# Reading scanned states in place in an S5 layer's output products

## The chip, the cores and the metric

The kernel runs on one core of one Trainium2 chip. The metric is device time in microseconds (us), from the start of the program to its end. A profiled execution also gives a trace with the instructions of each engine: PE (TensorE, with its weight loads as PEld), ACT (ScalarE), DVE (VectorE), POOL (GpSimd) and SP (SyncE, which issues most of the DMAs).

## The reference, cut to what matters

The program is an encoder of two layers on 256 tokens of width 2048, in float32. The first layer is attention; the change doesn't touch it. The second is a bidirectional S5 state-space layer, with a projection, a complex scan in each direction, an output product, a GELU, a gated unit and an output projection:

```
proj = einsum('bsd,de->bse', h, w_in);  u, z = split(proj, 2)
ug = u.reshape(b, s, 128 groups, 16 channels)
y_fwd = s5_direction(ug, ..., False);  y_bwd = s5_direction(ug, ..., True)
y = y_fwd + y_bwd + d_skip * u
g = gelu(y)
y = g * sigmoid(einsum('bse,ef->bsf', g, w_glu) + b_glu) * silu(z)
return einsum('bse,ed->bsd', y, w_out)
# s5_direction, with a state of 64 complex numbers per group:
bu = einsum('sbgc,gpc->sbgp', u, bb);  s[t] = a * s[t-1] + bu[t]
return einsum('gcp,sbgp->sbgc', c_re, s_re) - einsum('gcp,sbgp->sbgc', c_im, s_im)
```

## The kernel before

**Large products.** Each weight matrix is read in chunks of 512 KB. SP issues the load into `raw` (five buffers), ACT casts it into the high part `wh` (L146, three buffers), and POOL or DVE subtracts to get the low part `wl` (L148). PE then multiplies high by high, high by low and low by high: 24 matmuls with 256 columns for a chunk (L209 to L211). The S5 layer begins with 64 such chunks on `h1T`: four per block of 256 outputs, for u in chunks 0 to 31 and for the gate z in chunks 32 to 63. The GLU follows on `gT`, from chunk 64. Its first two blocks are interleaved: chunks 64 to 69 are quarters 0 to 2 of both, and chunk 70 is quarter 3 of the first, which needs the results of pieces 12 to 15. In chunks 1 to 69 it is POOL that makes `wl`. Six chunks of the last product (`w_out_ssm`) are loaded and split ahead of time into `kept`.

**The scan in pieces.** The sequence is cut into 64 slots of four tokens. The 128 groups form 16 pieces of eight. For each block of u, `ut` goes to DRAM (`Ud`, L841 and L842), and comes back as the right operand of `in_products` (L871), where PE makes the contributions of each slot to the states with 64x64 matmuls in four quarters of its array. ACT copies them into `V` (L875). `V` is laid out by slot, part (real or imaginary) and group, with one tile for pieces 0 to 7 and one for 8 to 15. The forward states lie on partitions 0 to 63, the backward states, with the order of the slots reversed, on 64 to 127. `scan_task` runs twice on DVE, once for each tile: per slot one product with the coefficients (L888) and two additions (L889, L890), each slot after the one before it.

**The outputs.** `out_task` makes one piece's outputs after its scan. Two copies (L908 on ACT; L909 on ACT, from piece 8 on DVE) and two memsets on POOL bring the states of the piece into `su`, shifted by a slot and with the backward part turned round. Sixteen matmuls `om` by `su` over 128 rows and eight `tt` by `up2` over 64 rows (L933) sum states and inputs in one bank of PSUM. ACT applies the GELU (L938) and issues the store to `Gd`; `g_task` reads that back as `gp` and splits it into `gT` (L243, L244). `tt` is a rearranged copy (L498) of eight 64 KB loads `tr` for every four pieces.

**What sets the order.** After each chunk a `step` advances the generators of the lanes in, scan, out and g, each by a step or a few. The out lane holds two tasks (`OUT_W`). The scan takes three slots per step. The `out_task`s of eight pieces are queued four steps (`OUT_LAG`) after their scan was written out, and a `g_task` waits in addition until no scan is left. A scheduler then puts each engine's instructions in one fixed order. Where an instruction waits, everything behind it on its engine waits too. `PSB` divides PSUM: three banks for the chunks, three for the pieces.

Of the kernel before, what the change touches and what calls it, by code (L numbers as in the profile page):

```python
# [18 lines left out]
S = 256  # L19
# [5 lines left out]
G = 128  # L25
# [15 lines left out]
class Trunk:  # L41
# [241 lines left out]
    def ssm_tables(self, tp, pp):  # L283
# [98 lines left out]
        self.coef = self.const.tile([128, 2, 2, G], F32, name="coef")  # L382
        nc.gpsimd.tensor_copy(self.coef[:, 0], pw[4][0].unsqueeze(1).to_broadcast([128, 2, G]))
        nc.gpsimd.tensor_copy(self.coef[:, 1, 0], pw[4][1])
        v.tensor_scalar(self.coef[:, 1, 1], pw[4][1], -1.0, None, ALU.mult)
# [101 lines left out]
    def toeplitz(self, b):  # L487

        nc, wk = self.nc, self.wk1
        raw = wk.tile([128, L, 16, C], F32, tag="q4", name="tr", bufs=self.Q4)  # L490
        with self.tc.issue_after(self.paced):
            for h in range(2):
                for tau in range(L):
                    src = self.Kd[b, h, :, 3 - tau:7 - tau].rearrange("c j e -> c (j e)")
                    nc.sync.dma_start(raw[h * 64 + tau:h * 64 + 64:L].rearrange("q j a e -> q (j a e)"), src)
        t = wk.tile([128, 16, C, L], F32, tag="tt", name="tt")
# [347 lines left out]
    def in_task(self, pc):  # L844
# [11 lines left out]
            yield  # L856
        self.small.append(lambda: self.in_products(pc, im, up))

    def in_products(self, pc, im, up):
        if pc == 8:  # L860
            self.V.append(self.s1.tile([128, NCH, 2, 64], F32, tag="s1", name="V"))
        nc, V, g0 = self.nc, self.V[pc // 8], pc % 8 * PG

        pss = [self.bank("vps").rearrange("p (g r s) -> p g r s", g=4, r=2) for _ in range(2)]
        with self.urgent() if self.IN_URG else ExitStack(), ExitStack() as order:
            for pr in range(4):
                for ri in range(2):
                    for hf, d in ((0, 0), (1, 1), (0, 1), (1, 0)):
                        h = slice(hf * 64, hf * 64 + 64)
                        mv = up[h, 1, pr] if d == 0 else up[h, 0, pr, ::-1]  # L870
                        m = nc.tensor.matmul(pss[hf][d * 64:d * 64 + 64, pr, ri], lhsT=im[h, pr, ri, d * 64:d * 64 + 64], rhs=mv, start=True, stop=True)  # L871
                        order.enter_context(self.tc.issue_after(m.ins))
        with self.urgent():
            for hf in range(2):
                nc.scalar.copy(V[:, :, :, g0 + hf:g0 + PG:2].rearrange("p s r g -> p g r s"), pss[hf])  # L875
        self.flags.add(("V", pc))

    def scan_task(self, p0, p1):

        v = self.nc.vector  # L880
        n, g0 = (p1 - p0) * PG, p0 % 8 * PG
        V = self.V[p0 // 8][:, :, :, g0:g0 + n]
        cf = self.coef[:, :, :, p0 * PG:p1 * PG]
        shp = [128, 2, 2, n]
        for c in range(1, NCH - 1):
            P = self.sc.tile([128, 512], F32, tag="scp", name="scp")[:, :4 * n].rearrange("q (e r g) -> q e r g", e=2, r=2)
            with self.urgent():
                v.tensor_tensor(P, cf, V[:, c - 1].unsqueeze(1).to_broadcast(shp), ALU.mult)  # L888
                v.tensor_tensor(V[:, c], V[:, c], P[:, 0], ALU.add)  # L889
                self.swept = v.tensor_tensor(V[:, c], V[:, c], P[:, 1, ::-1], ALU.add).ins  # L890
            yield
        t = self.now + self.OUT_LAG
        while self.now < t:
            yield
        for pc in range(p0, p1):
            self.add("out", self.out_task(pc))

    def out_task(self, pc):

        nc, v, wk = self.nc, self.nc.vector, self.wk1  # L900
        b, q = pc // 4, pc % 4
        V = self.V[pc // 8]
        gs = slice(pc % 8 * PG, pc % 8 * PG + PG)
        su = wk.tile([128, 2, PG, NCH], F32, tag="q4", name="su", bufs=self.Q4)
        f, r = slice(0, 64), slice(64, 128)
        nc.gpsimd.memset(su[f, :, :, 0:1], 0.0)  # L906
        nc.gpsimd.memset(su[r, :, :, NCH - 1:], 0.0)
        nc.scalar.copy(su[f, :, :, 1:], V[f, 0:NCH - 1, :, gs].rearrange("p s r g -> p r g s"))  # L908
        (v.tensor_copy if pc >= 8 else nc.scalar.copy)(su[r, :, :, :NCH - 1], V[r, NCH - 2::-1, :, gs].rearrange("p s r g -> p r g s"))  # L909
        self.flags.add(("su", pc))  # L910
        tag, bufs = ("im", self.NIM) if self.n_in == NPIECE and self.OMT else ("q4", self.Q4)
        om = wk.tile([128, 2, PG, C * L], F32, tag=tag, name="om", bufs=bufs)
        nc.sync.dma_start(om, self.OMd[pc])
        if q == 0:
            self.tt = self.toeplitz(b)
        tt = self.tt
        up = wk.tile([128, 4, NCH], F32, tag="up", name="up2", bufs=3)
        nc.sync.dma_start(up, self.Ud[pc].rearrange("h c t a k -> (h c t) a k"))
        yield
        yield  # L920
        ps = self.pm.tile([128, 512], F32, tag="pm", name="yps", bufs=self.npm)

        h = [slice(g % 2 * 64, g % 2 * 64 + 64) for g in range(PG)]
        o = [ps[h[g], g // 2 * NCH:g // 2 * NCH + NCH] for g in range(PG)]
        even, odd = range(0, PG, 2), range(1, PG, 2)
        jobs = [(g, None) for g in even] + [(g, ri) for ri in range(2) for g in range(PG)] + [(g, None) for g in odd]
        seen = set()
        with ExitStack() as order:
            for n, (g, ri) in enumerate(jobs):
                lhsT = tt[h[g], q * 4 + g // 2].rearrange("q e t -> q (e t)") if ri is None else om[:, ri, g]  # L930
                rhs = up[h[g], g // 2] if ri is None else su[:, ri, g]
                stop = ri is None if g % 2 else ri == 1
                m = nc.tensor.matmul(o[g], lhsT=lhsT, rhs=rhs, start=g % 2 not in seen, stop=stop, skip_group_check=True)  # L933
                seen.add(g % 2)
                order.enter_context(self.tc.issue_after(m.ins))
# [4 lines left out]
        self.add("g", self.g_task(pc), *[("su", p) for p in range(8)])  # L940

    def g_task(self, pc):

        nc, wk = self.nc, self.wk1
        yield

        while not self.idle("scan"):
            yield

        if self.gT is None:  # L950
            self.gT = self.s2.tile([128, 2, KB, S], F32R, tag="s2", name="gT")
        gp = wk.tile([128, S], F32, tag="gp", name="gp", bufs=6)
        nc.sync.dma_start(gp, self.Gd[pc].rearrange("g c t k -> (g c) (t k)"))
        for _ in range(self.GLAG):
            yield
        with self.tc.issue_after(self.mm) if self.GLAG > 2 else ExitStack(), self.tc.issue_after(self.swept):
            self.split(gp, self.gT[:, 0, pc], self.gT[:, 1, pc])
        self.flags.add(("g", pc))

    def glu_task(self, f, src, dst):  # L960
# [4 lines left out]
        gg = wk.tile([128, S], F32, tag="gp", name="gg", bufs=6)  # L965
# [7 lines left out]
    def open(self, ssm):  # L973
# [6 lines left out]
        cf = self.sc.tile([128, 2, 2, G], F32, name="cf")  # L980
        self.nc.scalar.copy(cf, self.coef)
        self.coef = cf
        self.V = [self.s2.tile([128, NCH, 2, 64], F32, tag="s2", name="V")]
        p0 = 0
        for p1 in self.BATCH:
            self.add("scan", self.scan_task(p0, p1), *[("V", p) for p in range(p0, p1)])
            p0 = p1
        self.flags.add("open")

    def layer1(self, out):  # L990
# [5 lines left out]
        self.gT, self.n_in = None, 0  # L996
# [135 lines left out]
    EACH = 2
# [56 lines left out]
```

## Time and profile before

| what | value |
|---|---|
| median of 3 runs | 916.02 us (911.74 to 917.16) |
| the profiled execution's own time | 910.61 us |
| its span | 908.4 us, so 2.2 us lie around it |
| mean granted clock of TensorE | 0.978 of full speed |
| busy share of the span | PE 93%, DVE 72%, ACT 57%, POOL 29% |
| HBM | 214 GB/s over the span |

Busy shares are means over stages of different kinds. The S5 layer's u blocks start a new piece about every four chunks from 440 us on. The last piece's `in_products` end at 560.8 us, and chunk 70 begins at 728.6 us; between these two the scans end and all outputs are made.

### The profile page before, as it was taken

What the parts mean: (1) busy time and instruction counts of PE and PEld (TensorE: products, weight loads), DVE (VectorE), ACT (ScalarE), POOL (GpSimd) and SP (SyncE); (2) the same over time, 40 slices, a digit from 0 to 9 for tenths busy, and PEclk for the clock granted to TensorE, in tenths of its full rate; (3) what the DMA queues carried; (4) which work ended last, traced back from release to release, by engine and by line L of the source; (5) the groups of instructions that cost most, each with busy time, mean ns of one, the idle gap of its engine ahead of it and who ended that gap; (6) DMA issues with size and microseconds to landing.
All of it is one profiled execution on the core that took longest, in us unless ns stands there. A gap on an engine that the chain in (4) does not pass through costs nothing.

```text
span 908.4 us, 18403 instructions
## 1 busy us (share of the span) xinstructions
PE 841.9 (93%) x7244; PEld 759.0 (84%) x7244; DVE 658.4 (72%) x1178; ACT 520.3 (57%) x743; POOL 263.4 (29%) x182
## 2 busy tenths in 40 slices
PE   5999999999999999997999999998898799999993
PEld 4788889989899787786889999987898699988872
DVE  3999899899979979967300798999632388756546
ACT  3554457778667674344566556489869464443321
POOL 0008500000001324433756666733684000000004
PEclk9999999999999999998999999998999989999997
DMA  9765587777767567987799899756886936777723
GB/s 228 239 192 180 142 255 212 246 187 227 187 199 199 181 178 235 240 280 251 234 261 272 256 290 283 198 152 179 241 257 206 314 123 210 231 237 242 236 50 92
DMA packets 217798, 195.82 MB, mean 216 GB/s; under 512 B 67648, under 2 KB 174064, under 8 KB 217456
## 3 DMA queue, kind: packets, MB, share of 16 engines
q1 hardware_dynamic: 200688, 189.93, 70.2%
q10 hardware_dynamic: 17024, 4.72, 2.2%
q8 instruction: 57, 0.93, 0.4%
q14 instruction: 29, 0.24, 0.1%
HBM read 168.39 MB, written 26.21 MB: 214 GB/s over the span
## 4 chain that ended last, share of the span: by engine, by line
PE 61%; DMA 13%; DVE 11%; issue 4%; ACT 4%; POOL 3%; SPq 2%; DVEq 0%; ACTq 0%; POOLq 0%
PE acc L209 10%; PE acc L211 10%; PE acc L210 10%; PE acc L185 8%; PE acc L186 8%; PE acc L184 8%; DVE wl L148 3%; DMA Ud<-ut 2%; PE yps L933 2%; PE vps L871 1%; DMA up<-Ud 1%; SPq L404 1%; PE kps L459 1%; DMA Gd<-yg 1%; DMA raw<-in_w_out_ssm_dram 1%
## 5 line engine op out<-in xcount | busy, mean ns | idle before, releaser
L146 ACT CAST wh<-raw 128x1024 fp32r<-128x1024 f32 x234 | 245.4, 1050 | 237.6 <-PE acc L186 98.8
L148 POOL TENSOR_TENSOR wl<-raw,wh 128x1024 fp32r<-128x1024 f32 x84 | 211.0, 2516 | 362.9 <-ACT wh L146 336.9
L148 DVE TENSOR_TENSOR wl<-raw,wh 128x1024 fp32r<-128x1024 f32 x150 | 190.8, 1276 | 52.9 <-ACT wh L146 51.9
L209 PE MATMUL acc<-h1T,wh 128*128 128x256 f32 x512 | 149.5, 294 | 3.4 <-ACT wh L146 1.8
L211 PE MATMUL acc<-h1T,wl 128*128 128x256 f32 x512 | 147.3, 288 | 5.7 <-POOL wl L148 5.7
L210 PE MATMUL acc<-h1T,wh 128*128 128x256 f32 x512 | 147.2, 288 | 0.0
L211 PEld LDWEIGHTS acc<-h1T,wl 128*128 128x128 f32 x512 | 100.4, 196 | 6.6 <-POOL wl L148 6.3
L888 DVE TENSOR_TENSOR scp<-cf,V 128x256 f32<-128x256 f32 x124 | 53.6, 433 | 71.2 <-ACT V L875 67.0
L209 PEld LDWEIGHTS acc<-h1T,wh 128*128 128x128 f32 x512 | 100.0, 196 | 5.9 <-ACT wh L146 2.1
L210 PEld LDWEIGHTS acc<-h1T,wh 128*128 128x128 f32 x512 | 100.4, 196 | 0.2 <-DVE h1T L836 0.2
L185 PE MATMUL acc<-wl,xT 128*128 128x512 f32 x192 | 76.6, 399 | 0.8 <-DVE wl L148 0.8
L209 PE MATMUL acc<-gT,wh 128*128 128x256 f32 x256 | 71.0, 288 | 5.8 <-ACT gT L243 5.1
L186 PE MATMUL acc<-wh,xT 128*128 128x512 f32 x192 | 76.0, 396 | 0.0
L184 PE MATMUL acc<-wh,xT 128*128 128x512 f32 x192 | 71.7, 400 | 2.7 <-ACT wh L146 2.7
L210 PE MATMUL acc<-gT,wh 128*128 128x256 f32 x256 | 73.4, 289 | 0.4 <-DVE gT L244 0.2
L211 PE MATMUL acc<-gT,wl 128*128 128x256 f32 x256 | 72.4, 287 | 0.4 <-POOL su L906 0.4
L209 PE MATMUL acc<-xT,wh 128*128 128x256 f32 x256 | 72.1, 285 | 0.0
L210 PE MATMUL acc<-xT,wh 128*128 128x256 f32 x256 | 71.8, 284 | 0.0
L211 PE MATMUL acc<-xT,wl 128*128 128x256 f32 x256 | 70.2, 286 | 1.1 <-DVE wl L148 1.1
L1096 POOL TENSOR_TENSOR r<-r,gains 128x512 f32<-128x512 f32 x8 | 11.0, 1404 | 186.8 <-ACT r L1094 186.7
L185 PE MATMUL acc<-wl,oT 128*128 128x512 f32 x128 | 51.6, 403 | 4.1 <-DVE wl L148 4.0
L209 PEld LDWEIGHTS acc<-gT,wh 128*128 128x128 f32 x256 | 48.3, 193 | 6.6 <-ACT gT L243 5.6
(254 smaller groups left out, 1880.4 us busy)
## 6 DMA issues: line engine op xcount, KB each, us to landing
raw<-in_w_in_attn_dram SPq DMA_DIRECT2D x80, 512.0 KB, 4.5
raw<-in_w_in_ssm_dram SPq DMA_DIRECT2D x64, 512.0 KB, 5.4
raw<-in_w_out_attn_dram SPq DMA_DIRECT2D x32, 512.0 KB, 5.7
raw<-in_w_glu_dram SPq DMA_DIRECT2D x32, 512.0 KB, 3.9
raw<-in_w_out_ssm_dram SPq DMA_DIRECT2D x32, 512.0 KB, 5.0
IMd<-im SPq DMA_DIRECT2D x16, 512.0 KB, 4.9
OMd<-om SPq DMA_DIRECT2D x16, 512.0 KB, 6.6
im<-IMd SPq DMA_DIRECT2D x16, 512.0 KB, 5.9
```

What stands on the lines that cost most here:

```text
L146: nc.scalar.copy(wh, raw)
L148: (nc.gpsimd if i - self.first in range(*self.POOL) or i in self.POOL0 else nc.vector).tensor_tensor(wl, raw, wh.bitcast(F32), ALU.subtract)
L184: nc.tensor.matmul(ps, lhsT=xh, rhs=wh[:, kk], start=kb == 0, stop=False)
L185: nc.tensor.matmul(ps, lhsT=xh, rhs=wl[:, kk], start=False, stop=False)
L186: nc.tensor.matmul(ps, lhsT=xl, rhs=wh[:, kk], start=False, stop=kb == KB - 1)
L209: nc.tensor.matmul(o, lhsT=wh[:, kk, f], rhs=ah[:, kb], start=kb == 0, stop=False)
L210: nc.tensor.matmul(o, lhsT=wh[:, kk, f], rhs=al[:, kb], start=False, stop=False)
L211: self.mm = nc.tensor.matmul(o, lhsT=wl[:, kk, f], rhs=ah[:, kb], start=False, stop=kb == KB - 1).ins
L404: nc.sync.dma_start(self.Bt[d * 64:d * 64 + 64, h, ri], a[bn][0, d, pc * PG + h * PG:pc * PG + h * PG + PG].rearrange("g p c -> p g c"))
L888: v.tensor_tensor(P, cf, V[:, c - 1].unsqueeze(1).to_broadcast(shp), ALU.mult)
L933: m = nc.tensor.matmul(o[g], lhsT=lhsT, rhs=rhs, start=g % 2 not in seen, stop=stop, skip_group_check=True)
L1096: (nc.gpsimd if k == "g" else v).tensor_tensor(x, x, o, op)
```

## The change

`V` is laid out by group, slot and part, so that a real and an imaginary number are neighbours and the slots of a group lie 8 bytes apart. Slot 0 is set to zero, and the scan goes over slots 2 to 63. The output matmuls read `V` where it lies: the forward half with a stride of two numbers, the backward half likewise and from the end. `su`, its copies and its memsets are gone.

The matmuls of a piece become 64x64: eight for `tt` (two quarters in turn) and 32 for the states (four quarters in turn). A row half of the array sums into its own bank. One step after the matmuls ACT copies the second bank (L950), which a step later DVE adds to the first (L952), and another step later ACT applies the GELU (L954).

The `out_task`s are queued when the pieces' buffers are opened, not after the scan. Up to three of them (`OUT_W`) load `om`, `tr` and `up2` early, wait for the flag `states`, and then start one per step. The copy of `tr` into `tt` is now in `turned`. `PSB` is (2, 4), and `up2` has buffers of its own.

```diff
 def in_products(self, pc, im, up):
...
-                nc.scalar.copy(V[:, :, :, g0 + hf:g0 + PG:2].rearrange("p s r g -> p g r s"), pss[hf])
+                nc.scalar.copy(V[:, g0 + hf:g0 + PG:2, 1:].rearrange("p g s r -> p g r s"), pss[hf][:, :, :, :NCH - 1])
 def scan_task(self, p0, p1):
...
-        for c in range(1, NCH - 1):
+        for c in range(2, NCH):
...
-                v.tensor_tensor(P, cf, V[:, c - 1].unsqueeze(1).to_broadcast(shp), ALU.mult)
-                v.tensor_tensor(V[:, c], V[:, c], P[:, 0], ALU.add)
-                self.swept = v.tensor_tensor(V[:, c], V[:, c], P[:, 1, ::-1], ALU.add).ins
+                v.tensor_tensor(P, cf, V[:, :, c - 1].unsqueeze(1).to_broadcast(shp), ALU.mult)
+                v.tensor_tensor(V[:, :, c], V[:, :, c], P[:, 0], ALU.add)
+                self.swept = v.tensor_tensor(V[:, :, c], V[:, :, c], P[:, 1, :, ::-1], ALU.add).ins
...
-        for pc in range(p0, p1):
-            self.add("out", self.out_task(pc))
+        self.flags.add(("states", p0 // 8))
 def out_task(self, pc):
...
-        nc.scalar.copy(su[f, :, :, 1:], V[f, 0:NCH - 1, :, gs].rearrange("p s r g -> p r g s"))
-        (v.tensor_copy if pc >= 8 else nc.scalar.copy)(su[r, :, :, :NCH - 1], V[r, NCH - 2::-1, :, gs].rearrange("p s r g -> p r g s"))
...
+        while ("states", pc // 8) not in self.flags or pc and ("out", pc - 1) not in self.flags or self.out_at == self.now:
+            yield
+        self.out_at = self.now
+        if q == 0:
+            self.tt = self.turned(b, tr)
...
-        jobs = [(g, None) for g in even] + [(g, ri) for ri in range(2) for g in range(PG)] + [(g, None) for g in odd]
+        jobs = [(m, m, pr, None) for pr in range(4) for m in range(2)]
+        jobs += [(d, m, pr, ri) for pr in range(4) for ri in range(2) for d, m in ((0, 0), (1, 1), (0, 1), (1, 0))]
...
-        nc.scalar.activation(yg.rearrange("p a k -> p (a k)"), ps[:, :S], AF.Gelu_apprx_tanh)
+        nc.scalar.copy(y, pss[1][:, :S])
+        yield
+        v.tensor_tensor(y, y, pss[0][:, :S], ALU.add)
+        yield
+        nc.scalar.activation(y, y, AF.Gelu_apprx_tanh)
```

The first place is ACT around the casts of chunks 48 to 50, where the first scan's pieces get their outputs. Here it is before:

```order
L146 CAST wh_7427<-raw_7305 128x1024
L1034 ACTIVATE z1_6633<-acc0_7304 128x256
L146 CAST wh_7497<-raw_7356 128x1024
L908 COPY su_7282<-V_5000 64x16x63
L909 COPY su_7282<-V_5000 64x16x63
L908 COPY su_7347<-V_5000 64x16x63
L909 COPY su_7347<-V_5000 64x16x63
L908 COPY su_7540<-V_5000 64x16x63
L909 COPY su_7540<-V_5000 64x16x63
L908 COPY su_7593<-V_5000 64x16x63
L909 COPY su_7593<-V_5000 64x16x63
L146 CAST wh_7553<-raw_7425 128x1024
```

The same place on ACT after the change; the last row is again the cast of chunk 50:

```order
L146 CAST wh_7570<-raw_7352 128x1024
L950 COPY yg_7522<-yps_7395 128x256
L954 ACT_TABLE_LOAD
L954 ACTIVATE yg_7522<-yg_7522 128x256
L955 DMA Gd_4711<-yg_7522 128x4x64
L950 COPY yg_7524<-yps_7437 128x256
L954 ACTIVATE yg_7524<-yg_7524 128x256
L955 DMA Gd_4711<-yg_7524 128x4x64
L950 COPY yg_7612<-yps_7527 128x256
L954 ACTIVATE yg_7612<-yg_7612 128x256
L955 DMA Gd_4711<-yg_7612 128x4x64
L146 CAST wh_7618<-raw_7480 128x1024
```

In place of eight copies of states, three copies from PSUM and three GELUs now stand ahead of the cast of chunk 50. Each of these GELUs reads the result of an addition on DVE. The first such addition stands on DVE inside a slot of the second scan (after 79 of the two scans' 124 slots; the second and third after 82 and 87):

```order
L898 TENSOR_TENSOR scp_7169<-cf_4998,V_5955 128x256
L952 TENSOR_TENSOR yg_7522<-yg_7522,yps_7394 128x256
L899 TENSOR_TENSOR V_5955<-V_5955,scp_7169 128x64x2
L900 TENSOR_TENSOR V_5955<-V_5955,scp_7169 128x64x2
L898 TENSOR_TENSOR scp_7173<-cf_4998,V_5955 128x256
```

The additions for the pieces 3 to 7 stand after slots 99, 108, 111, 120 and 124, and the GELUs of 4 and 5 ahead of the cast of chunk 57, that of 6 ahead of the cast of chunk 59. On PE the matmuls of pieces 0 to 2 stand within chunk 47, those of 3 to 15 from chunk 51 to chunk 66 (before: 0 to 7 from chunk 48 to chunk 59, and 8 to 15 from chunk 65 to chunk 70).

The second place is ACT at the end of the outputs. Before, the last two pieces read like this:

```order
L938 ACTIVATE yg_8767<-yps_8738 128x256
L939 DMA Gd_4711<-yg_8767 128x4x64
L146 CAST wh_8940<-raw_8872 128x1024
L243 CAST gT_8259<-gp_8765 128x256
L938 ACTIVATE yg_8799<-yps_8770 128x256
L939 DMA Gd_4711<-yg_8799 128x4x64
L146 CAST kept_10348<-raw_10300 128x1024
```

And after the change:

```order
L950 COPY yg_9023<-yps_8978 128x256
L146 CAST kept_10574<-raw_10526 128x1024
L146 CAST kept_10574<-raw_10528 128x1024
L146 CAST kept_10574<-raw_10530 128x1024
L954 ACTIVATE yg_9023<-yg_9023 128x256
L146 CAST wh_9066<-raw_8936 128x1024
L955 DMA Gd_4711<-yg_9023 128x4x64
L146 CAST wh_9100<-raw_9032 128x1024
L243 CAST gT_8369<-gp_9096 128x256
```

Three casts into `kept` now stand between the copy of piece 15 and its GELU, and the casts of chunks 69 and 70 around the store of its result. One of the three raws lies in a buffer that an `om` of the last pieces holds until its matmuls end.

## Rows read from the trace of the kernel before

**Rows 1.** Busy time of each engine in stretches (us), with the granted clock.
```profile
core 0: us, PE busy (x) PEld busy (x) DVE busy (x) ACT busy (x) POOL busy (x), PEclk, DMA share, GB/s
560.80:728.60 167.80, 148.79 (x1610) 140.48 (x1609) 104.51 (x253) 121.19 (x126) 85.91 (x62) 0.96 0.75 224
600.00:640.00 40.00, 31.59 (x344) 29.07 (x340) 36.28 (x109) 39.00 (x32) 12.13 (x13) 0.87 0.56 164
...
730.00:732.00 2.00, 2.00 (x10) 2.00 (x11) 0.83 (x3) 0.34 (x1) 0.00 (x0) 0.50 0.00 0
```
**Rows 2.** Chain of waits: start, duration (us), step, its instructions.
```profile
559.71 1.09 PE vps L871 x64
...
643.51 2.29 PE yps L933 x48
...
674.78 0.60 PE yps L933 x8
```
**Rows 3.** Timeline of PE within a chunk: start, duration, instruction.
```profile
673.66 0.28 PE L210 MATMUL acc<-h1T,wh 128*128 128x256 f32 x1
673.78 0.28 PE L211 MATMUL acc<-h1T,wl 128*128 128x256 f32 x1
```
**Rows 4.** Groups of ACT, 590 to 735 us: busy, mean ns, idle before.
```profile
L908 ACT COPY su<-V 64x1008 f32<-64x1008 f32 x16 | 31.6, 1992 | 0.1
...
L909 ACT COPY su<-V 64x1008 f32<-64x1008 f32 x8 | 15.9, 1991 | 0.1
L938 ACT ACT_TABLE_LOAD x5 | 6.4, 1283 | 0.1
...
L938 ACT ACTIVATE yg<-yps 128x256 f32<-128x256 f32 x16 | 6.0, 382 | 6.2 <-DMA Gd<-yg 3.0 <-PE yps L933 1.8 <-PE acc L211 0.5
```
**Rows 5.** Timelines of ACT, POOL and PE around chunk 50.
```profile
594.70 2.07 ACT L908 COPY su<-V 64x1008 f32<-64x1008 f32 x1
...
610.79 1.04 ACT L146 CAST wh<-raw 128x1024 fp32r<-128x1024 f32 x1
...
611.96 2.36 POOL L148 TENSOR_TENSOR wl<-raw,wh 128x1024 fp32r<-128x1024 f32 x1 [10.84 <-PE yps L933]
...
614.38 0.39 PE L211 MATMUL acc<-h1T,wl 128*128 128x256 f32 x1 [1.79 <-POOL wl L148]
```
**Rows 6.** Timeline of DVE: the scans' first slot, two of their last.
```profile
504.52 0.43 DVE L888 TENSOR_TENSOR scp<-cf,V 128x256 f32<-128x256 f32 x1 [65.15 <-ACT V L875]
...
641.85 0.43 DVE L888 TENSOR_TENSOR scp<-cf,V 128x256 f32<-128x256 f32 x1
...
642.96 0.43 DVE L888 TENSOR_TENSOR scp<-cf,V 128x256 f32<-128x256 f32 x1
...
643.75 0.29 DVE L890 TENSOR_TENSOR V<-V,scp 128x128 f32<-128x128 f32 x1
```
**Rows 7.** Groups of DVE over the whole span.
```profile
L909 DVE COPY su<-V 64x1008 f32<-64x1008 f32 x8 | 13.6, 1721 | 13.5 <-ACT tt L498 10.6 <-issue 1.5 <-PE yps L933 1.3
```
**Rows 8.** Timeline of ACT, its queue and PE: the last piece's result on its way.
```profile
718.54 0.38 ACT L938 ACTIVATE yg<-yps 128x256 f32<-128x256 f32 x1 [0.71 <-PE yps L933]
718.96 0.42 ACTq L939 DMA_DIRECT2D Gd<-yg  x1
...
728.59 1.22 PE L209 MATMUL acc<-gT,wh 128*128 128x256 f32 x4 [1.28 <-ACT gT L243]
```
**Rows 9.** Timeline of ACT when the first piece comes.
```profile
456.70 2.01 ACT L875 COPY V<-vps 128x512 f32<-128x512 f32 x2 [0.68 <-ACT ut L841]
```
**Rows 10.** Issued DMAs: KB each, median us to landing.
```profile
raw<-in_w_out_ssm_dram SPq DMA_DIRECT2D x32, 512.0 KB, 5.0
...
tr<-Kd SPq DMA_DIRECT2D x32, 64.0 KB, 3.2
```
**Rows 11.** Busy time while the first pieces come in.
```profile
440.00:480.00 40.00, 36.20 (x543) 34.78 (x545) 0.00 (x0) 21.48 (x27) 27.89 (x12) 1.00 0.85 243
```
**Rows 12.** One line of ACT: durations of a copy out of PSUM (ns).
```profile
L841 ACT COPY ut<-acc x16: 365/366/374, 440.5 to 546.5; 128x256 f32<-128x256 f32 x16
```

More of the change, by code (lines that the diff above doesn't have):

```diff
@@ L380, in ssm_tables @@
                             nc.gpsimd.tensor_copy(self.op[i][b, :, c, :, 3 - k], src[b])
[L382 to L385, printed above, removed]
+        self.coef = self.const.tile([128, 2, G, 2], F32, name="coef")
+        nc.gpsimd.tensor_copy(self.coef[:, 0], pw[4][0].unsqueeze(2).to_broadcast([128, G, 2]))
+        nc.gpsimd.tensor_copy(self.coef[:, 1, :, 0], pw[4][1])
+        v.tensor_scalar(self.coef[:, 1, :, 1], pw[4][1], -1.0, None, ALU.mult)
     def ssm_scratch(self):
@@ L495, in toeplitz, with turned @@
                     nc.sync.dma_start(raw[h * 64 + tau:h * 64 + 64:L].rearrange("q j a e -> q (j a e)"), src)
-        t = wk.tile([128, 16, C, L], F32, tag="tt", name="tt")
+        return raw
+    def turned(self, b, raw):
+        nc, wk = self.nc, self.wk1
+        tag, bufs = ("im", self.NIM) if b > 1 and self.n_in == NPIECE else ("tt", 1)
+        t = wk.tile([128, 16, C, L], F32, tag=tag, name="tt", bufs=bufs)
         for a in range(2):
@@ L910, in out_task @@
-        self.flags.add(("su", pc))
-        tag, bufs = ("im", self.NIM) if self.n_in == NPIECE and self.OMT else ("q4", self.Q4)
-        om = wk.tile([128, 2, PG, C * L], F32, tag=tag, name="om", bufs=bufs)
+        om = wk.tile([128, 2, PG, C * L], F32, tag="q4", name="om", bufs=self.Q4)
         nc.sync.dma_start(om, self.OMd[pc])
         if q == 0:
-            self.tt = self.toeplitz(b)
-        tt = self.tt
-        up = wk.tile([128, 4, NCH], F32, tag="up", name="up2", bufs=3)
-        nc.sync.dma_start(up, self.Ud[pc].rearrange("h c t a k -> (h c t) a k"))
@@ L919, in out_task @@
[L919 to L925, printed above, removed]
-        jobs = [(g, None) for g in even] + [(g, ri) for ri in range(2) for g in range(PG)] + [(g, None) for g in odd]
-        seen = set()
-        with ExitStack() as order:
[L929 to L935, printed above, removed]
+            tr = self.toeplitz(b)
@@ new lines, in out_task @@
+        up = wk.tile([128, 4, NCH], F32, tag="up2", name="up2", bufs=3)
+        nc.sync.dma_start(up, self.Ud[pc].rearrange("h c t a k -> (h c) t a k"))
+        yield
[5 more added lines that the diff above has]
+            yield
+            yield
+        tt = self.tt
+        V = self.V[pc // 8][:, pc % 8 * PG:pc % 8 * PG + PG]
@@ new lines, in out_task @@
+        half = [slice(0, 64), slice(64, 128)]
+        jobs = [(m, m, pr, None) for pr in range(4) for m in range(2)]
+        jobs += [(d, m, pr, ri) for pr in range(4) for ri in range(2) for d, m in ((0, 0), (1, 1), (0, 1), (1, 0))]
+        pss, seen = [self.bank("yps") for _ in range(2)], set()
+        with ExitStack() as order:
+            for r, m, pr, ri in jobs:
+                g = 2 * pr + m
+                if ri is None:
+                    w, x = tt[half[r], q * 4 + pr].rearrange("q e t -> q (e t)"), up[half[r], pr]
+                else:
+                    w, x = om[half[r], ri, g], V[half[r], g, ::-1 if r else 1, ri]
+                i = nc.tensor.matmul(
+                    pss[r][half[m], pr * NCH:pr * NCH + NCH], lhsT=w, rhs=x,
+                    start=(r, m) not in seen, stop=ri == 1, skip_group_check=True,
+                )
+                seen.add((r, m))
+                order.enter_context(self.tc.issue_after(i.ins))
@@ L936, in out_task @@
+        self.flags.add(("out", pc))
         yield
         yg = wk.tile([128, 4, NCH], F32, tag="yg", name="yg", bufs=2)
-        nc.scalar.activation(yg.rearrange("p a k -> p (a k)"), ps[:, :S], AF.Gelu_apprx_tanh)
+        y = yg.rearrange("p a k -> p (a k)")
+        nc.scalar.copy(y, pss[1][:, :S])
+        yield
+        v.tensor_tensor(y, y, pss[0][:, :S], ALU.add)
+        yield
+        nc.scalar.activation(y, y, AF.Gelu_apprx_tanh)
         nc.scalar.dma_start(self.Gd[pc].rearrange("(a h) c t k -> (h c t) a k", h=2), yg)
-        self.add("g", self.g_task(pc), *[("su", p) for p in range(8)])
+        self.add("g", self.g_task(pc), *[("out", p) for p in range(8)])
@@ L979, in open @@
         self.psum(*self.PSB)
[L980 removed]
+        cf = self.sc.tile([128, 2, G, 2], F32, name="cf")
         self.nc.scalar.copy(cf, self.coef)
         self.coef = cf
[L983 removed]
+        self.V = []
+        self.new_states(self.s2, "s2")
         p0 = 0
@@ L987, in open @@
             p0 = p1
+        for pc in range(NPIECE):
+            self.add("out", self.out_task(pc), ("V", pc // 8 * 8))
         self.flags.add("open")
@@ L1122 @@
     POOL0 = range(80, 110, 2)
-    PSB = (3, 3)
+    PSB = (2, 4)
     OPEN = 99
@@ L1126 @@
     POOL = (1, 70)
-    OUT_W = 2
+    OUT_W = 3
     OUT_E = 1
-    OMT = 1
     IN_EVERY = 1
```

25 lines of the change are left out of this document (11 added, 14 removed).

## The prediction

> **What bounds the kernel now.** I read the busy time by stretches first, then the chain of waits, then the groups and timelines of the engines that it names. Between the end of the last piece's input products (559.71 + 1.09 = 560.8 us) and the first matmul of chunk 70 (728.59) lie 167.8 us, of which PE is busy 148.8 [rows 1, 2, 8]. PE is the bound, with 19 us of gaps. The work itself is less than its busy time: matmuls of a chunk follow each other every 0.12 us [rows 3], so that one of 24 takes 2.87, and 34 chunks (36 to 69) 97.6; the 16 pieces take 2.29 each [rows 2], 36.6. Together 134.2. So 33.6 us are to be explained: the 19 of gaps, the rest changes of mode and lost clock. From 600 to 640 us PE's granted clock is 0.87 and its gaps are 8.4 us, with ACT busy 39.0 of 40 [rows 1]; a two-microsecond stretch at 0.50, that is 1.2 GHz, follows directly on the long wait before chunk 70 [rows 1]. There ACT is the cause: eight copies of 2 us, the first at 594.70, put off the cast of chunk 50 to 610.79; POOL had waited 10.84 us before its `wl` at 611.96, and PE 1.79 until 614.38 [rows 5]. The last such wait is that for piece 15: GELU at 718.54, store issued at 718.96, chunk 70 at 728.59 [rows 8], so 9.6 us from the issue to PE.
>
> **The change, part by part.** I rebuild PE's time from 560.8 us on, in the changed order.
>
> *The products.* A float32 matmul has two records in the trace: x64 are the 32 products of `in_products`, x8 four of `tt`. Thirty-two 64x64 products in four quarters take 1.09 [rows 2], as the new state products should; four `tt` products of one quarter take 0.60 [rows 2], and two quarters in turn I put at the same 0.60. A piece then costs 1.69 in place of 2.29: 16 x 0.60 = 9.6 us less on PE. What the trace doesn't show is a right operand that is read with a stride of two numbers; the bounds are 1.69 and, if quarters no longer overlap, 32 x 0.15 + 0.60 = 5.4. I take 1.69, since the backward operand of `in_products`, read from its end, is already part of the 1.09.
>
> *ACT and DVE.* Sixteen plus eight copies of 1.99 us go from ACT, 47.5 us, and eight of 1.72 from DVE [rows 4, 7]. Sixteen copies from PSUM of 0.37 each [rows 12] come to ACT, 5.9 us. GELU and SiLU alternate more often, with 14 table loads in place of 10: 4 x 1.28 = 5.1 [rows 4]. ACT has 36 us less to do. DVE gets 16 additions, each about as long as a 256-wide product of the scan, 0.43 [rows 6]; the eight for the first scan's pieces lengthen the second scan by 3.4. The memsets and their waits on POOL cost nothing now or then: POOL was waiting for ACT.
>
> *The scan.* Slots come every 1.11 us (641.85 to 642.96) [rows 6]. The two scans ran from 504.52 to 644.04: 124 x 1.11 and a pause of some 1.8. Their operands become pairs of numbers 512 bytes apart. From the two sizes of operation, 0.43 for 256 and 0.29 for 128 numbers per partition [rows 6], a number costs about 1.1 ns and an operation 0.15 us. The one DVE row that reads single numbers 512 bytes apart, the copy of 1008 in 1721 ns [rows 7], comes to 1.56 ns. For the 512 numbers of a slot that is +0.22 us at the upper end and 0 at the lower; nothing speaks for a gain, since the operands lay in a row before. I take 0, as a pair still gives two numbers per step, and keep the other end as a rival. The Trainium skill, "SBUF — State Buffer", section "Specifications (TRN2)", states 16-byte lines of which at least two hits are needed for full bandwidth; a pair of float32 is two hits, so by it a slot stays at 1.11, while the trace of before has no row with pairs at all.
>
> *The early loads.* Now 4 `om` (512 KB), 8 `tr` (64 KB) and 3 `up2` (128 KB), some 2.9 MB, are issued on SP among the inputs of the first pieces, where the DMA engines are busy 0.85 and move 243 GB/s [rows 11]: 11.9 us of transfer at that rate. Where spare DMA time takes all of it up, nothing is lost; where none does, 11.9. The copy of `tr` into `tt` also stands on ACT ahead of the first copy into `V`, at 456.70 before [rows 9], and waits for eight loads with 3.2 us to landing [rows 10]. I take a delay of 6, half of the transfers: the share of 0.85 leaves 6 of 40 us free. So chunk 36 begins at 566.8 and the scan at 510.5.
>
> *The outputs of the first scan.* From chunk 36, 11.4 chunks (32.7) and then pieces 0 to 2 (5.1) end at 604.6; chunk 50 is reached 2.6 chunks later, 612.1. Its cast stands behind the GELU of piece 2, and that behind the third addition, after 87 slots: 510.5 + 96.6 + 1.8 + 1.3 = 610.2. With a GELU of 0.38 [rows 4], a cast of 1.04 and a `wl` of 2.36 [rows 5], `wl` is there at 614.0; PE asks for it at 612.3, a wait of 1.7. The same sum gives 1.1 at chunk 57 (addition of piece 5 after 111 slots, 638.0) and 3.0 at chunk 59 (piece 6, after 120 slots, 648.4). These 5.8 replace the 8.4 of gaps and the low clock between 600 and 640.
>
> *The second scan.* It ends at 510.5 + 137.6 + 1.8 + 3.4 = 653.3. PE reaches chunk 62, where pieces 8 and 9 stand, at 660.8: 7.5 us of room.
>
> *The end of the outputs.* Four chunks and eight pieces later, at 685.8, piece 15 is done. Now three casts into `kept` stand before its GELU on ACT, and one of their raws can be loaded only when the last pieces' matmuls have released its buffer: 5.0 for the load [rows 10], about two casts, a table load and the GELU, and the cast of chunk 69 before the store is issued, near 695.1. With the 9.6 from issue to PE, chunk 70 begins at 704.7; before, it was 728.6. The store thus goes out 9 us after the matmuls, where it took about 2 before. These are given away here, and still 23.9 us remain: 9.6 of shorter pieces, 20 of waits and clock, less 6 for the loads. After chunk 70 nothing changes. The sum goes against the profiled execution: 910.6 - 23.9 = 886.7. The median of the runs is 5.4 above that execution, so the forecast is **892**, with 885 to 901 of its own.
>
> **Rivals.** *More of it comes through* (24 in 100). The early loads find room, and ACT is ahead everywhere: without the 6 and the 5.8 chunk 70 begins at 692.9, 35.7 earlier, 880 (872 to 886). For it: the `om` loads taken early are not made later. Against it: SP's queue is a fixed order, and the share in 440 to 480 is already 0.85 [rows 11].
>
> *The scan pays for its stride* (14). At 1.33 us per slot, the price of single numbers [rows 7], the scans end at 680. PE then waits at chunk 62, and chunk 70 comes 11.5 (chunks 62 to 65) + 13.5 (eight pieces) + 18.9 later, at 724: about 912, no change. The GELUs of the first scan come late as well, but what PE loses there it would wait at chunk 62 anyway. For it speaks that the row is of the same engine and the same distance; against it the pair.
>
> *Slower: the scan pays double* (5). ACT's copies of single numbers take 1.97 ns per number [rows 4], nearly twice what its cast of 1024 in 1.04 us does [rows 5]. If DVE did the same to its pairs, a slot would be 1.11 + 0.53 us, the scans would end 66 us later, near 719, and chunk 70 begin at 763: 950. It turns slower from 1.36 us per slot on, where the 7.5 of room and the 23.9 of gain are used up (31.4 over 124 slots).
>
> *The change doesn't do what it says* (5). If a strided right operand keeps the quarters from working beside each other, a piece takes 5.4; 16 x 3.7 = 59 us, of which the waits hide some 6, so about 945. It turns slower from 3.6 us per piece on. Against it: quarters do overlap in `in_products` at 0.034 us per product.
>
> The Trainium skill, "TensorEngine Tiling (Array Packing)", section "PSUM Bottleneck", says that tiling speeds up TensorE but not the emptying of PSUM, which may become the bottleneck. By the rows, copy, addition and GELU of a piece are 0.37 + 0.43 + 0.38 = 1.2 us on two engines against 1.69 on PE, so by their length they don't; by their places in ACT's and DVE's order they cost the 5.8 above.
>
> **How the numbers follow.** The forecast has 52 in 100. The range of 873 to 914 takes in the forecast, most of the first rival and most of the second; it leaves out the two slow ones and the ends of the others, some 18 in 100. A measurement of this kernel can tell about 1% from no change, 9 us: the forecast and the first rival are faster by more than that (76), the second rival is the same (14), the last two are slower (10).
>
> **What would show it in the profile after.** Right: the 32 state products and eight `tt` of a piece in about 1.7 us; no copies of states on ACT, 14 table loads; slots of 1.11 us and scans that end near 653; at chunks 50 and 59 PE waiting for POOL's `wl` behind a GELU that waits for DVE; chunk 70 near 705, ahead of it the casts into `kept` and the GELU of piece 15; a DMA share over 0.9 in 440 to 480. Wrong: slots over 1.2 with PE waiting at chunk 62 for the scan; pieces over 2.5; the first scan more than 8 us later than 504.5; or a granted clock that falls in new places, since the shorter pieces leave PE's new waits without work around them. The forecast is most exposed at the end of the outputs, where one late raw holds ACT and everything behind it.

## The result and the profile after

The changed kernel takes 920.0 us (916.95 to 923.23, 9 runs) against 912.07 (911.49 to 917.16, 9 runs); the ratio is 1.0079, with a 95% interval of 1.0057 to 1.0100. It is slower by 0.8%, where 892 had been forecast, 2.6% below the 916.02 of the first three runs. Its profiled execution took 921.98 us with a span of 920.2, 11.8 more than before.

The parts of the change itself did what was expected of them. Timeline of PE in the changed kernel, two pieces in a row:

```profile
679.47 0.62 PE L940 MATMUL yps<-up,tt 64*64 64x64 f32 x14
679.88 0.28 PE L940 MATMUL yps<-V,om 64*64 64x64 f32 x2
679.92 0.22 PE L940 MATMUL yps<-up,tt 64*64 64x64 f32 x2
679.98 1.10 PE L940 MATMUL yps<-V,om 64*64 64x64 f32 x62
680.92 0.57 PE L940 MATMUL yps<-up,tt 64*64 64x64 f32 x14
```

From one piece to the next are 1.45 us (679.47 to 680.92), where 2.18 stood before (two pieces in a row, 702.91 to 705.09 us; the 2.29 of [rows 2] are one piece from start to end). `tt` overlaps with the states. The strided operand costs nothing: the 62 records of the states take 1.10 us, as the 64 of `in_products` do [rows 2]. Timeline of DVE, the last two slots:

```profile
655.18 0.43 DVE L898 TENSOR_TENSOR scp<-cf,V 128x256 f32<-128x256 f32 x1
655.65 0.30 DVE L899 TENSOR_TENSOR V<-V,scp 128x128 f32<-128x128 f32 x1
655.98 0.29 DVE L900 TENSOR_TENSOR V<-V,scp 128x128 f32<-128x128 f32 x1
656.31 0.43 DVE L898 TENSOR_TENSOR scp<-cf,V 128x256 f32<-128x256 f32 x1
```

A slot takes 1.13 us, against 1.11 [rows 6]. Groups of ACT from 590 to 740 us:

```profile
L954 ACT ACTIVATE yg<-yg 128x256 f32<-128x256 f32 x16 | 6.7, 417 | 12.8 <-DVE yg L952 12.7
L503 ACT COPY tt<-tr 128x512 f32<-128x512 f32 x6 | 6.5, 1128 | 7.3 <-DMA tr<-Kd 7.3
L243 ACT CAST gT<-gp 128x256 fp32r<-128x256 f32 x16 | 6.1, 406 | 30.2 <-DMA gp<-Gd 30.2
L950 ACT COPY yg<-yps 128x256 f32<-128x256 f32 x16 | 5.9, 370 | 6.2 <-PE yps L940 2.6 <-DMA Gd<-yg 2.6 <-ACT yg L954 1.0
```

The copies of states [rows 4] are gone. What grew are the waits of the casts into `gT` for reads of pieces: ACT stood still before them for 30.2 us. In the kernel before (590 to 735 us) it was 4.7:

```profile
L243 ACT CAST gT<-gp 128x256 fp32r<-128x256 f32 x16 | 6.0, 402 | 4.7 <-DMA gp<-Gd 4.5
```

Busy time by stretches:

```profile
core 0: us, PE busy (x) PEld busy (x) DVE busy (x) ACT busy (x) POOL busy (x), PEclk, DMA share, GB/s
600.00:640.00 40.00, 35.24 (x642) 33.91 (x642) 32.05 (x97) 22.23 (x30) 20.61 (x9) 0.91 0.69 202
680.00:720.00 40.00, 21.51 (x532) 20.25 (x529) 3.89 (x9) 11.55 (x20) 6.47 (x3) 0.74 0.46 142
692.00:694.00 2.00, 2.00 (x11) 2.00 (x11) 0.41 (x2) 1.50 (x3) 0.00 (x0) 0.50 0.98 280
```

From 600 to 640 us the gaps of PE fell from 8.4 [rows 1] to 4.8. From 680 to 720 PE now stands still for 18.5 of 40 us, and from 692 to 694, after its wait of 8.64 us, the granted clock is at 0.50, 1.2 GHz. What it waits for is seen in the timelines of PE and ACT; here is the one long wait of the earlier stretch, and then the lines of the last pieces, in order of time:

```profile
618.76 0.58 PE L209 MATMUL acc<-h1T,wh 128*128 128x256 f32 x1 [4.10 <-ACT z L1053]
686.08 2.04 ACT L503 COPY tt<-tr 128x512 f32<-128x512 f32 x2 [6.75 <-DMA tr<-Kd]
691.12 0.58 PE L209 MATMUL acc<-gT,wh 128*128 128x256 f32 x1 [8.64 <-ACT z L1053]
702.68 0.40 ACT L243 CAST gT<-gp 128x256 fp32r<-128x256 f32 x1 [7.55 <-DMA gp<-Gd]
702.74 0.37 ACTq L955 DMA_DIRECT2D Gd<-yg  x1
708.01 0.40 ACT L243 CAST gT<-gp 128x256 fp32r<-128x256 f32 x1 [4.92 <-DMA gp<-Gd]
709.26 0.36 ACT L950 COPY yg<-yps 128x256 f32<-128x256 f32 x1
709.68 1.46 PE L940 MATMUL yps<-up,tt 64*64 64x64 f32 x15 [8.27 <-ACT yg L950]
710.56 0.37 ACTq L955 DMA_DIRECT2D Gd<-yg  x1
715.55 0.41 ACT L243 CAST gT<-gp 128x256 fp32r<-128x256 f32 x1 [5.02 <-DMA gp<-Gd]
715.86 0.37 ACT L950 COPY yg<-yps 128x256 f32<-128x256 f32 x1
721.55 0.41 ACT L243 CAST gT<-gp 128x256 fp32r<-128x256 f32 x1 [4.36 <-DMA gp<-Gd]
728.06 0.41 ACT L243 CAST gT<-gp 128x256 fp32r<-128x256 f32 x1 [3.32 <-DMA gp<-Gd]
733.32 0.37 ACTq L955 DMA_DIRECT2D Gd<-yg  x1
```

The cast into `gT` of a piece stands ahead of the next piece's copy out of PSUM (L950). The cast waits until its piece was added, put through GELU, stored to DRAM and read back; the casts of pieces 11 to 14 begin at 708.01, 715.55, 721.55 and 728.06. Each piece thus pays a whole round trip of 6 to 7.5 us in turn. PE waits 8.27 us, until the copy at 709.26, for the bank that it empties. The other long wait of this stretch, 8.64 us ahead of chunk 64 (691.12), ends with a SiLU (L1053), which stands on ACT behind the copy of the last `tr`; that copy had waited 6.75 us for its loads. The store of the last piece goes out at 733.32; before it was 718.96 [rows 8]. In ACT's order of the changed kernel this stood to be read:

```
L243 CAST gT_8369<-gp_8926 128x256
L146 CAST wh_8938<-raw_8567 128x1024
L950 COPY yg_8870<-yps_8783 128x256
L954 ACTIVATE yg_8870<-yg_8870 128x256
L955 DMA Gd_4711<-yg_8870 128x4x64
L243 CAST gT_8369<-gp_8973 128x256
L950 COPY yg_8872<-yps_8825 128x256
```

Here `gp_8926` and `gp_8973` are pieces 11 and 12, `yg_8870` and `yg_8872` pieces 12 and 13. One more line matters: in the prediction 728.59 [rows 8] is called the first matmul of chunk 70. By the count of matmuls, 24 to a chunk from chunk 64 on, the first one in the kernel before is this:

```profile
718.44 0.74 PE L209 MATMUL acc<-gT,wh 128*128 128x256 f32 x4
```

728.59 is a place where that product stands still for the last pieces, 24 matmuls later. The cast (L243) that PE waits for at 728.59 began at 728.14 behind casts into `kept`, which had themselves waited for loads; the 9.6 us from store to PE are therefore not the round trip alone. Below the store of piece 15 is compared.

### The profile page after: what moved, and what is told of

It is laid out like the page before. It is cut to its first block, busy times and chain, and to the rows that moved or that the text cites. A ratio compares the mean times of both kernels' runs of the same rounds, so it can differ in the third digit from the quotient of the medians.

```text
span 920.2 us, 19362 instructions
## 1 busy us (share of the span) xinstructions
PE 839.9 (91%) x7756; PEld 760.1 (83%) x7756; DVE 656.1 (71%) x1186; ACT 470.5 (51%) x739; POOL 253.6 (28%) x152
## 4 chain that ended last, share of the span: by engine, by line
PE 61%; DMA 14%; DVE 13%; issue 4%; ACT 3%; SPq 3%; POOL 1%; ACTq 0%; DVEq 0%; POOLq 0%
PE acc L209 10%; PE acc L211 10%; PE acc L210 10%; PE acc L185 8%; PE acc L186 7%; PE acc L184 7%; DVE wl L148 3%; DMA raw<-in_w_out_ssm_dram 2%; DMA Gd<-yg 2%; PE vps L881 2%; DMA im<-IMd 2%; DMA Ud<-ut 2%; PE yps L940 1%; PE kps L459 1%; SPq L404 1%
## 5 line engine op out<-in xcount | busy, mean ns | idle before, releaser
L148 POOL TENSOR_TENSOR wl<-raw,wh 128x1024 fp32r<-128x1024 f32 x84 | 206.4, 2461 | 420.2 <-ACT wh L146 409.7
L209 PE MATMUL acc<-gT,wh 128*128 128x256 f32 x256 | 75.7, 296 | 12.0 <-ACT z L1053 8.6
L210 PE MATMUL acc<-gT,wh 128*128 128x256 f32 x256 | 74.7, 292 | 0.0
L209 PEld LDWEIGHTS acc<-gT,wh 128*128 128x128 f32 x256 | 51.4, 201 | 12.8 <-ACT z L1053 8.8
```

The lines of the kernel that those rows point to most:

```text
L148: (nc.gpsimd if i - self.first in range(*self.POOL) or i in self.POOL0 else nc.vector).tensor_tensor(wl, raw, wh.bitcast(F32), ALU.subtract)
L209: nc.tensor.matmul(o, lhsT=wh[:, kk, f], rhs=ah[:, kb], start=kb == 0, stop=False)
L210: nc.tensor.matmul(o, lhsT=wh[:, kk, f], rhs=al[:, kb], start=False, stop=False)
```

## The experiments

All times are medians; ratios are to the kernel before on the same chip. Theory A is the chain of round trips just read. Its rivals: B, the last `tr`, which is issued on SP only from 675.84 us on, so that its copy holds ACT and the SiLU behind it until chunk 64 can begin (8.64 us); C, the early loads, which put off all pieces; D, the two PSUM banks that the chunks have left; E, the casts into `kept` ahead of the last GELU.

**Casts into `gT` behind the stores.** From piece 8 on a cast is issued after the store of the piece two later:

```diff
-        with self.tc.issue_after(self.mm) if self.GLAG > 2 else ExitStack(), self.tc.issue_after(self.swept):
+        n = min(pc + 2, NPIECE - 1)
+        while pc >= 8 and n not in self.sent:
+            yield
+        with self.tc.issue_after(self.mm) if self.GLAG > 2 else ExitStack(), self.tc.issue_after(self.swept if pc < 8 else self.sent[n]):
```

> The casts into gT of pieces 8 to 15 are put behind the store of the piece two later on ACT; nothing else is changed. Theory A (in the changed kernel, the copy of each piece from 12 on stands behind the cast of the piece before it, which waits for a store and a load through DRAM, some 6 us per piece): copies of pieces 12 to 15 follow their matmuls, the 8.3 us wait of PE for a bank goes, chunk 70 begins 12 to 20 us earlier than 739.9, 900 to 908 us. Theory B (the late load of the last tr is what costs): the wait of 8.6 us before chunk 64 stays and with it the time, 918 to 921. Theory C (the early loads): as B, 918 to 921.

Measured: 904.98 us, 0.9902 (0.9872 to 0.9932). Theory A holds: one order on ACT is worth 15 us (16 by the ratios), and turns the change into a gain of 1%. The wait at chunk 64 is 4.89 us here. Timeline of ACT in this kernel:

```profile
699.59 0.37 ACT L950 COPY yg<-yps 128x256 f32<-128x256 f32 x1
700.95 0.37 ACTq L955 DMA_DIRECT2D Gd<-yg  x1
704.32 0.37 ACT L950 COPY yg<-yps 128x256 f32<-128x256 f32 x1 [0.35 <-DMA Gd<-yg]
705.62 0.37 ACTq L955 DMA_DIRECT2D Gd<-yg  x1
...
716.54 0.37 ACTq L955 DMA_DIRECT2D Gd<-yg  x1
```

The last store goes out at 716.54, 16.8 us earlier than in the changed kernel; 1.6 of these lie ahead of the scan, in work that the edit doesn't touch (PE's first wait for `ut` ended at 443.26, in the changed kernel at 444.89).

**Four buffers for `yg`** (`bufs=2` to `bufs=4`), the rival that blames the buffers for the chain:

> The changed kernel with four buffers for yg in place of two, and the casts into gT where they stand. A rival of theory A: not the casts but the two buffers (a copy waits for the store of the piece two before it) make the chain of round trips; then 902 to 910 us. Theory A: the casts stand where they stood and the time stays, 917 to 921.

Measured: 922.59 us, 1.0105 (1.0058 to 1.0152). The buffers aren't it; the casts stand where they stood.

**Five buffers for `om` and `tr`** (`Q4 = 5`), so that the last `tr` can be loaded earlier:

> Five buffers in place of four for om and tr (Q4), nothing else is written differently. Theory B: the tr loads of pieces 12 to 15 are issued before 675 us, the copy into tt no longer stands still, PE doesn't wait 8.6 us at chunk 64, 911 to 913 us. Theory A: the round trips from piece 10 to 15 stay; as they begin only after this copy, between 0 and 8 us come through, 912 to 920. If the time stays at 918 or above, neither the wait at chunk 64 nor the tr load is on the path.

Measured: 919.67 us, 1.0071 (1.0047 to 1.0094). The wait at chunk 64 fell from 8.64 to 4.51 us and the median hardly moved. The chain is still there, and PE waits 7.12 us for a bank behind it; that it took the gain back is argued, not shown.

**Three and three banks** (`PSB = (3, 3)`):

> Three PSUM banks for the chunks and three for the pieces, as before the change. If a theory D holds (two banks for the chunks make PE wait for SiLU's reads), the wait of 8.6 us before chunk 64 shrinks to below 3 and the time falls to 911 to 915. Theory A: three banks hold one and a half pieces, PE waits more often for a copy, and the round trips stay; 920 to 930.

Measured: 910.28 us, 0.9966 (0.9937 to 0.9994). That looked like theory D. The wait of 4.10 us at 618.76 is gone, and that at chunk 64 is 2.56. But in this kernel the scheduler also set another order on ACT, in which the copy of piece 15 no longer stands behind the cast of piece 14, but waits for PE:

```profile
719.93 0.38 ACT L950 COPY yg<-yps 128x256 f32<-128x256 f32 x1 [0.49 <-PE yps L940]
```

Both edits together tell them apart:

> The casts into gT behind the stores, as in the first experiment, and three and three banks. Theory D (two banks for the chunks cost PE time of their own: 8.6 us before chunk 64, 4 between 600 and 640) says that the two gains add: 905 - 10 = 893 to 898 us. Theory A (with three banks the scheduler put fewer copies behind round trips, which is what made that kernel faster) says that this gain is already taken: 902 to 908.

Measured: 904.15 us, 0.9919 (0.9892 to 0.9946), the same as without the banks. D falls as a cost of its own: its wait of 4.10 us is gone here too, waits of 0.9 to 1.9 us between 633 and 661 us stand in other places, and the gain of 10 us was part of A's 15.

**The loads later.** The output tasks are queued when the last piece of their scan has come in, or the last of all:

```diff
-            self.add("out", self.out_task(pc), ("V", pc // 8 * 8))
+            self.add("out", self.out_task(pc), ("V", pc // 8 * 8 + 7))
```
```diff
+            self.add("out", self.out_task(pc), ("V", 15))
```

> The output tasks are queued when the last piece of their scan has come in, not the first: om, tr and up2 are no longer loaded among the first pieces' inputs. Theory C: the first slot of the scan comes back from 512.3 to 504 to 506, and all that follows is 6 to 8 us earlier, 912 to 914 us. Theories A and B: the scan starts earlier too, but om and tr come late for pieces 0 to 2 and the round trips at the end stay; 914 to 922.

> The changed kernel with its output tasks queued when the last of all 16 pieces has come in: om, tr and up2 of pieces 0 to 2 are loaded near 560 to 575 us, as before the change. Theory C (the early loads delay the first pieces and with them everything): the scan starts at 504 to 506 in place of 512.3 and all later work moves with it, 912 to 915 us. If the start moves and the time doesn't (918 or more), the round trips at the end take the gain back.

Measured: 925.68 us, 1.0127 (1.0086 to 1.0167), and 924.09, 1.0120 (1.0060 to 1.0179). Both are no faster, and theory C in this form falls. In the first the scan begins later still, at 514.9 in place of 512.3. In the second it begins at 507.7, but the eight `tr` loads, which keep SP for 6.2 us, and the copy that waits 7.49 us for them on ACT stand in the way at their new place too:

```profile
560.00:600.00 40.00, 34.99 (x321) 33.98 (x320) 26.72 (x80) 16.99 (x23) 23.83 (x11) 0.91 0.67 196
```

In the kernel before and in the changed kernel PE has no gap there, here it has 5.0 us; in the first of the two runs it has 5.2 us of waits at 512 to 514 us, again behind such a copy. The loads cost some 5 us wherever these edits put them.

**After A, the others one by one.** All of these have the casts behind the stores.

> The casts into gT behind the stores, and five buffers for om and tr. Theory B in the form that is left (the late tr load costs once the round trips are gone): the wait of 4.9 us before chunk 64 goes, 899 to 902 us. If A alone is the cause of all the loss, 903 to 907.

Measured: 900.14 us, 0.9877 (0.9837 to 0.9917). The wait at chunk 64 is 2.04 us here. Against the first experiment the median is 4.8 us lower and the ratio 0.25%, 2 to 3 us; the two intervals overlap, so this run alone doesn't show B.

> The casts into gT behind the stores, and the casts into kept behind the store of piece 15, which no longer waits for a load of w_out_ssm that stands behind three reads of pieces on SP. Theory E (the end of the outputs, as the prediction had it, gives away 6 us there): the store goes out near 711 in place of 716.5 and chunk 70 begins some 4 to 6 us earlier, 899 to 902 us. If the cast of chunk 69, which now stands behind the same load, is what PE waits for, 903 to 907.

The casts into `kept` were issued after the store of piece 15 (`issue_after(self.sent[NPIECE - 1])`). Measured: 904.30 us, 0.9915 (0.9887 to 0.9942), no change: E falls in this form. The store of piece 15 does go out at 710.42, but the cast of chunk 69, behind the same load, stays where it was (716.51, in the first experiment 716.41). The same with three and three banks:

> All three: gT casts behind the stores, kept casts behind the store of piece 15, three and three banks. D and E together: 888 to 893 us. A alone: 902 to 907. D alone 893 to 898, E alone 899 to 902.

Measured: 905.68 us, 0.9915 (0.9876 to 0.9954). Five buffers and the later `kept` casts, five buffers and the later loads, and these with four `yg` buffers:

> gT casts behind the stores, five buffers, and the casts into kept behind the store of piece 15. If the casts into kept hold piece 15's GELU (706.7 to 714.1 us in the kernel without this edit) and nothing else is as late, chunk 70 begins 4 to 6 us earlier, 894 to 897 us. If the cast of chunk 69 behind the same load takes it back, as it did with four buffers, 899 to 902.

> gT casts behind the stores, five buffers, and the loads after the last input piece. If the three terms (round trips 15, late tr 4, early loads 6 to 8) add up, 892 to 895 us, which is the time that was forecast; if the early loads only filled time that is lost elsewhere, 899 to 902.

> gT casts behind the stores, five buffers for om and tr, loads after the last input piece, and four buffers for yg. With the casts out of the way the two buffers of yg may be the next wait (2.6 to 2.9 us in single places): 889 to 893 us. If they are hidden, as the kernel without this edit, 892 to 895.

Measured: 901.68 us, 0.9846 (0.9776 to 0.9916); 902.80, 0.9878 (0.9827 to 0.9928); 902.90, 0.9883 (0.9837 to 0.9930). They lie between 900 and 905 as well; no further gain is seen.

**No round trips at all.** Pieces 8 to 15 read what was stored for pieces 0 to 7, so that no read waits for a store just made. The output is no longer the layer's; the amount of work and of traffic is:

```diff
-        nc.sync.dma_start(gp, self.Gd[pc].rearrange("g c t k -> (g c) (t k)"))
+        nc.sync.dma_start(gp, self.Gd[pc % 8].rearrange("g c t k -> (g c) (t k)"))
```

> The changed kernel, but the reads of pieces 8 to 15 take the stored results of pieces 0 to 7, so that none of them waits for a store just made (the second half of the GLU's input is replaced by the first half's; the amount of work and of traffic is the same). Theory A (round trips through DRAM between the pieces): all of them go, that of the last piece too, which the kernel before has as well (9.6 us): 888 to 898 us. If the pieces at the end are late for another reason (ACT's own work, banks, late loads), 908 or more.

> gT casts behind the stores, five buffers, and reads that need no store, as in the run above (the same part of the data replaced). ACT's order at the end stays that of the kernel without this edit. If SP's waits for stores are what is left, up2 of piece 15 and the load of w_out_ssm come 4 to 8 us earlier, 890 to 896 us. If PE's and ACT's own work is what is left, 898 to 902.

Measured: 906.03 us, 0.9929 (0.9902 to 0.9956), and 902.59, 0.9883 (0.9828 to 0.9937). The first, with the casts not moved by hand, lies 1 us above what A alone gave: by two different edits the round trips explain 14 to 16 us. (Here the scheduler itself set all casts of pieces 8 to 15 ahead of the copies of pieces 10 to 15.) Timeline of PE in the first:

```profile
694.41 0.58 PE L209 MATMUL acc<-gT,wh 128*128 128x256 f32 x1 [9.13 <-ACT z L1053]
```

The wait ahead of chunk 64 is still whole there. So `tr` got a buffer of its own and was loaded one block ahead, with the casts behind the stores (two places of the edit):

```diff
-        raw = wk.tile([128, L, 16, C], F32, tag="q4", name="tr", bufs=self.Q4)
+        raw = wk.tile([128, L, 16, C], F32, tag="tr", name="tr", bufs=1)
...
+            if b < 3:
+                self.trs[b + 1] = self.toeplitz(b + 1)
```

> gT casts behind the stores; tr has a buffer of its own and is loaded right after the copy of the tr before it, so the last one near 660 us in place of 676 to 682. Theory B in its last form (the late tr holds ACT, SiLU and PE at chunk 64): that wait is below 1 us, 895 to 900 us. If the wait goes and the time stays at 903 to 907, what follows at the end makes up for it.

> The same with the casts into kept behind the store of piece 15. If after tr the end of the outputs is next (piece 15's GELU behind the casts into kept), 890 to 896 us; if the cast of chunk 69 takes it back, as in the two runs with this edit, the same as the kernel without it.

Measured: 901.48 us, 0.9874 (0.9839 to 0.9908), and 901.89, 0.9882 (0.9856 to 0.9907). Timeline of PE in the first of the two:

```profile
643.69 0.47 PE L944 MATMUL yps<-V,om 64*64 64x64 f32 x2 [4.48 <-issue]
...
688.14 0.39 PE L209 MATMUL acc<-gT,wh 128*128 128x256 f32 x1 [1.02 <-ACT z L1060]
...
694.05 0.62 PE L944 MATMUL yps<-up,tt 64*64 64x64 f32 x14 [1.28 <-DMA up<-Ud]
699.46 0.62 PE L944 MATMUL yps<-up,tt 64*64 64x64 f32 x14 [3.79 <-DMA up<-Ud]
```

The wait at chunk 64 is 1.0 us, and the time is 3.5 us below that of the first experiment. Next PE waits for loads of `up2`, and a wait of 4.48 us at 643.69 is new. Taken together the runs do show B: the four kernels with the casts behind the stores and nothing done about `tr` lie at ratios of 0.990 to 0.992 (28 runs), the seven with five buffers or the early `tr` as well at 0.985 to 0.988 (28 runs). That is about 3 us.

## Why the prediction was wrong

*The products* were right, and cheaper than taken: 1.45 us per piece, not 1.69, because `tt` overlaps with the states.

*The scan* was right: 1.13 us per slot, and 0.43 for the product of 256 numbers, as before [rows 6]. The trace agrees with the sentence quoted from the Trainium skill, "SBUF — State Buffer", "Specifications (TRN2)", by which at least two hits per 16-byte line are needed for full bandwidth. The rivals that let the scan pay are out. So is the one with quarters that don't overlap.

*The early loads*: 6 was taken, and the first slot came 7.8 later (512.3 for 504.5). But 2.7 of these lie ahead of the first of the loads (453.46): PE's first wait in this layer, for `ut`, ended at 444.89 in place of 442.16, and between the executions of all these kernels that time differs by up to 4 us. The loads cost 5.1, so the size was near. The reason given for it, transfers that find no room, isn't shown: the DMA share from 440 to 480 us was 0.86, not over 0.9, and in the two runs with later loads the 5 us are waits behind a copy of `tr`.

*The outputs of the first scan*: gaps of 4.8 us from 600 to 640, against 5.8 taken to 660. That the size was near is luck. The GELUs do wait for DVE's additions, ACT stood still 12.7 us for them, but PE doesn't wait for POOL's `wl` at chunks 50 and 59. Of the 4.8 us 4.10 are one wait at 618.76, for a SiLU that stands behind the GELU of piece 2 and sets free one of the two banks that the chunks have left; the prediction had no term for these banks. The second scan's last operation ended at 657.4, 4.1 us after its forecast of 653.3, and piece 8 began at 666.4, 5.6 after its forecast of 660.8.

*The end of the outputs* is the step that failed. It reads "Four chunks and eight pieces later, at 685.8, piece 15 is done": PE's work alone was added up from chunk 62 on, with no term for any wait, on the ground that copy, addition and GELU take less than PE's products. Piece 15 was done at 718.4, so 52.0 us later than piece 8 began, not 25.0. Of the 27 us more, 20.9 are waits of PE: 8.64 behind the late `tr`, 8.27 for the bank behind the chain of round trips, and 4.0 in three smaller places; most of the rest are matmuls at 1.2 GHz after these waits. The store followed 14.9 us after, against 9.3, again behind the chain. So the store came 38.2 us after its forecast of 695.1: 5.6 ahead of piece 8, 27.0 in the pieces 8 to 15, 5.6 behind them. The term after it, 9.6 from store to PE, didn't act as forecast either: chunk 70 begins near 740.3, 7.0 after the store, when piece 15 has already been cast (737.38). The last long wait of PE before it is for the cast of chunk 69, which stands on ACT behind the casts into `kept`:

```profile
734.28 0.58 PE L209 MATMUL acc<-gT,wh 128*128 128x256 f32 x1 [2.67 <-ACT wh L146]
```

The order of instructions showed a cast into `gT` ahead of every one of the last copies; what was worked out from it were three casts into `kept` at its end. In the kernel before there was such a chain too, but with two pieces more of slack: the GELU of piece 15 stood behind the cast of piece 12, and waited 0.71 us, for PE [rows 8].

*Two smaller errors* stand in the sum itself. At 728.59, taken for the first matmul of chunk 70, 24 matmuls or 2.9 us of this work were already done; so the 33.6 us to be explained are 30.7, and the gain of 23.9 was put 2.9 too high. And the 5.4 added for the median came from three runs; with the 912.07 of nine runs the forecast gain gives 888, not 892.

The miss in the gain is thus 32 us: 23.9 were forecast, and 7.9 were lost. The runs account for 14 to 16 of them by the order of the casts (A) and for about 3 by the late `tr` (B), which counts only once A is gone; 3 are the misread matmul. Some 10 us stay open. The waits for `up2` make 5 in the profile of the kernel with the early `tr`, and stretches at 1.2 GHz have a share, but no run separated these. The two rivals that ended slower, by the scan and by the quarters, were right in sign and wrong in mechanism.

## What to carry to other kernels

Where a result goes out to DRAM and comes back, look at which instruction of an in-order engine waits for it, and at what stands behind that one: if it is the next item's first step, every item pays the round trip in turn. Shares of busy time don't show this; the two lines of the order do. And when work that filled an engine's queue is removed, the scheduler can set what is left in an order in which such a chain appears.

## What was not expected of the hardware

The time of a copy on ACT changed with the stride with which it writes. The copies of contributions from PSUM into `V`, of 512 numbers 512 bytes apart, took 1123 ns (first line, kernel before, L875); with 504 numbers 8 bytes apart they take 627 (second line, kernel after, L885). DVE's scan, which went the other way, from a row to pairs 512 bytes apart, stayed the same: 0.43 us for a product of 256 numbers in both kernels.

```profile
L875 ACT COPY V<-vps 128x512 f32<-128x512 f32 x32 | 32.4, 1123 | 10.4 <-PE vps L871 5.9 <-ACT ut L841 4.3
```
```profile
L885 ACT COPY V<-vps 128x504 f32<-128x504 f32 x32 | 18.2, 627 | 13.1 <-PE vps L881 6.7 <-ACT ut L846 4.2 <-DMA up<-Ud 2.2
```
